# A butterfly with scaled sums on ScalarE, silu gates behind the transform, and a reordered output phase in an FNet and Hyena encoder layer

## The chip, the cores and the metric

One core of a Trainium2 chip runs the whole layer in one launch. The metric is the time of one execution in device microseconds. Five engines have queues of their own, each worked through in order: PE (TensorE, matmuls), DVE (VectorE), ACT (ScalarE), POOL (GpSimd) and SP, which here only issues DMAs. An instruction that waits holds back everything behind it in its own queue.

## The reference, cut to what matters

Two sequences of 1024 rows and 1024 channels pass through the same layer:

```
p = rmsnorm(x) @ w_in                     # split into fv, fg, hv (3 parts), hg, mg
y_f = (fft2(fv).real * silu(fg)) @ w_fourier_out
v, x1, x2 = short_conv(hv)                # width 3 along the sequence
z = v
for n, gate in enumerate((x1, x2)):
    z = gate * (irfft(rfft(z, 2L) * kf[:, n])[:L] + hyena_d[n] * z)
y_h = (z * silu(hg)) @ w_hyena_out
g_f, g_h = split(sigmoid(mg + b_merge))
out = x + rmsnorm((g_f * y_f + g_h * y_h) @ w_out)
```

`kf` is the spectrum of a filter that a small network makes from positions. All of it is fp32.

## The kernel before, in words

PE multiplies fp32 as a high and a low part. `split` (line 168) makes them: ACT casts the high part (line 171, "CAST" in the profile; the names end in h: wh, yh, bh), then DVE or POOL subtracts the low part (line 181; wl, yl, bl). `mm3` then needs three matmuls per product. So each operand passes through two engines before PE may use it.

The phases follow one another, the first index b being the sequence. (1) The Fourier branch, to 225 us. (2) 16 filter steps, to about 650 us; each makes one block of filter taps and transforms it. (3) `branches` (line 905): 32 convolution steps, 16 of b=0 to about 1110 us and 16 of b=1 to about 1700 us. Step i runs `conv_front` for i+1 (the transform's input), `gates` for i+1 (the multiplier `x` of the step, line 923), and then `conv_back` for i: matmuls into `pX`, DVE's products `t` and `y`, the split of `y` into `yh` and `yl`, and matmuls into `pT` that use these. (4) `phase_gates`, to about 1940 us: what is left of the gate projections, as block products with seven multiplications in place of eight ("jobs"). (5) `phase_out` (line 1095): for four units (b, half) the projections by w_fourier_out (`pyf`, operand `sf`) and w_hyena_out (`pyh`, operand `sh`), eight blocks `dt` each; each block loads two weight tiles `wr` by DMAs that POOL issues (line 1123), which `split` turns into `wh`, `wl`; then a sigmoid gate `g` is read back from DRAM by a DMA of SP (line 1151) and put through ACT (line 1153). (6) `last_rows` (line 1245), from 2302 us: eight jobs that multiply by w_out, again with seven multiplications, `po`, and write the rows.

`butterfly` (line 546) is called 48 times in the phases 2 and 3, once for each step. It takes the eight blocks of 128 columns of a transform's input (`xp`, and `xm` for the part that is subtracted: another tile in the 16 filter steps, `bs2` holding its sums; the same tile `xt` in the 32 convolution steps) and makes four groups b0 to b3 of four blocks. b1 and b3 are e ± C8·d and similar, eight `scalar_tensor_tensor` of 128 columns (line 177), each with the constant C8 inside. Groups 1 to 3 are split for the matmuls into `pX`.

In `gates`, the second convolution (n=1) of sequence 0 also multiplies `x` by silu of a gate. The gate lies in DRAM for the channels below NH; one half at a time, SP loads it into a tile "gt" of three buffers (line 935), ACT puts it through silu in place (line 937), and POOL multiplies. The silu is held behind `self.turned`, a mark of the filter phase.

What sets the order: a scheduler rearranges the program's instructions before they are fixed in each queue; `tc.issue_after(ins)` keeps an instruction behind a given one on its own engine, and costs no wait by itself. Tiles of one tag share their buffers, so that a new tile waits until the old one is used up. Two of these sharings matter: in `phase_gates`, `kept` (line 1052) puts copies of products in the tag "w" of two buffers, in which `phase_out` puts its first `wr`; the last copy is used up by the last `gt`.

`phase_out` prepares `last_rows` by the way: `beside` (line 1162) loads a block of w_out, splits it and its sums (`blocks`, line 1185), a quarter of the blocks at a time; in the last unit `sum4` (line 1208) loads the tiles T4 (`t4l`) from DRAM and splits them. In `last_rows`, `prepare` (line 1254) loads `mraw` by DMA and splits it for the next job; `kept` copies products out of PSUM (line 1286, `m` and `u`).

Of the kernel before, what the change touches and what calls it, by code (L numbers as in the profile page):

```python
# [161 lines left out]
class K:  # L162
# [5 lines left out]
    def split(self, h, l, src, eng="pool", heng="act"):  # L168
        nc = self.nc
        if heng == "act":  # L170
            self.rounded = nc.scalar.copy(h, src)  # L171
        else:
            nc.vector.tensor_copy(h, src)
        self.sub(eng, l, src, h)
# [4 lines left out]
    def tt(self, eng, out, a, b, op):  # L179
        e = self.nc.gpsimd if eng == "pool" else self.nc.vector  # L180
        e.tensor_tensor(out, a, b, op=op)  # L181
# [4 lines left out]
    def sub(self, eng, out, a, b):  # L186
        self.tt(eng, out, a, b, SUB)
# [359 lines left out]
    def butterfly(self, ws, xp, xm):  # L547
# [7 lines left out]
        b0, b2, b1, b3 = t("b0"), t("b2"), t("b1"), t("b3")  # L555
        out = {0: b0}

        def split(g, b):
# [3 lines left out]
            out[g] = (h, l)  # L562
        self.add("dve", s, xp[:, :, 0:2], xp[:, :, 2:4])
        self.add("dve", b0[:, 0::2], s[:, :, 0], s[:, :, 1])
        self.sub("dve", b0[:, 1::2], s[:, :, 0], s[:, :, 1])
        self.sub("dve", b2[:, 0:2], xp[:, 0, 0:2], xp[:, 0, 2:4])
        self.sub("dve", b2[:, 2], xp[:, 1, 3], xp[:, 1, 1])
        self.sub("dve", b2[:, 3], xp[:, 1, 0], xp[:, 1, 2])
        split(2, b2)
        if xm is xp:  # L570
            de, do, sgn = b2[:, 1], b2[:, 2], -1.0
            se, so = s[:, 0, 1], s[:, 1, 1]
        else:
# [333 lines left out]
    def branches(self, nb, nct, ws):  # L907
# [11 lines left out]
        Z, X = {}, {}  # L919
# [6 lines left out]
        def gates(i):  # L926
            b, n, c = steps[i]
            x = self.conv(2 + n, c, ws, f"x{n + 1}", b)
            if n and b == 0:
                early = c < NH  # L930
                ps = None if early else self.inproj(4, c)
                for q in range(2):
                    sg = self.wp.tile([P, 512], F32, tag="gt", name="sg", bufs=3)
                    if early:
                        nc.sync.dma_start(sg, self.d_g[0][4][c][:, 512 * q:512 * q + 512])
                    with tc.issue_after(self.turned.ins):
                        nc.scalar.activation(sg, sg if early else ps[:, 512 * q:512 * q + 512], AF.Silu)
                    self.mul("pool", x[:, 512 * q:512 * q + 512], x[:, 512 * q:512 * q + 512], sg)
            X[i] = x
        B = front(0)  # L940
        gates(0)
        for i, (b, n, c) in enumerate(steps):
# [6 lines left out]
            y = self.conv_back(n, c, B, ws)  # L949
            B = nxt  # L950
# [31 lines left out]
    def phase_gates(self):  # L982
# [6 lines left out]
        with ExitStack() as es:  # L989
# [62 lines left out]
            def kept(p, own=False):  # L1052
                t = gw.tile([P, 512], F32, tag="u", name="u", bufs=1) if own else wp.tile([P, 512], F32, tag="w", name="m", bufs=2)
# [12 lines left out]
            for i, (sec, c) in enumerate(jobs):  # L1066
# [6 lines left out]
                v = kept(pa)  # L1073
# [17 lines left out]
    def phase_out(self):  # L1091
# [6 lines left out]
        with ExitStack() as es:  # L1098
# [17 lines left out]
            def weight(w, dt, q):  # L1116
# [10 lines left out]
                self.weighed = self.rounded  # L1127
# [34 lines left out]
            def beside(i, dt):  # L1162

                with tc.issue_after(self.fetched.ins), tc.issue_after(self.opened.ins):
                    if i in (1, 2):
# [3 lines left out]
                        elif part == 3:  # L1169
                            blocks(k, self.raw)  # L1170
# [15 lines left out]
            def blocks(k, r):  # L1186
# [6 lines left out]
                self.sums(s, r)  # L1193
# [245 lines left out]
```

## Time and profile before

| | us |
|---|---|
| three runs, median | 2466.59 |
| lowest to highest | 2461.57 to 2469.35 |
| the profiled execution, its own time | 2470.75 |
| its span in the profile | 2469.0 |

The profiled execution lies 4.16 us above the median; 1.75 us of its time lie around the span. In the profile a row of a view gives an engine, a line of the kernel, the operation, out<-in by the names above and the shape. Where an engine stood idle before a row, brackets give the idle time and what ended it.

### The profile page before, as it was taken

The page shows a single profiled execution, that of the slowest core. Times are in us where ns is not written, and L with a number is a line of the kernel's source. Part 1 is how long each engine was busy: PE and PEld are TensorE (multiplying, and loading weights), DVE is VectorE, ACT ScalarE, POOL GpSimd, SP SyncE. Part 2 cuts the span into 40 slices and gives each one's busy share as a digit, 9 for nine tenths or more (in the row PEclk, how much of TensorE's full clock was granted, in tenths as well). Part 3 has the DMA queues.
Part 4 walks back from the last instruction along what each step waited for, and adds up shares of the span by engine and source line. Part 5 has one row for each costly group of instructions (what it writes and reads, how often), then busy time and mean ns, then how long its engine had stood idle before and what let it go on. Part 6 is the DMA issues. An engine that isn't in the chain of part 4 may idle for free.

```text
span 2469.0 us, 36969 instructions
## 1 busy us (share of the span) xinstructions
PE 2407.5 (98%) x13196; PEld 2086.9 (85%) x13196; DVE 1912.8 (77%) x3597; ACT 1064.4 (43%) x1919; POOL 499.0 (20%) x516
## 2 busy tenths in 40 slices
PE   6999999999999999999999999999999999999998
PEld 6988888888788888888888888888788788787786
DVE  7687898998649999899889999866556455665677
ACT  5546576766433333333222222323444344444343
POOL 1331213221342443331000000112100111112121
PEclk9999999999999999999999999999999999999999
DMA  7535655555555455545443443435444567775443
GB/s 274 183 122 205 217 182 166 169 180 168 171 174 179 159 176 163 172 149 203 137 134 131 143 142 131 133 128 176 161 162 158 193 218 255 237 268 194 156 160 128
DMA packets 225153, 429.37 MB, mean 174 GB/s; under 512 B 23542, under 2 KB 87255, under 8 KB 224456
## 3 DMA queue, kind: packets, MB, share of 16 engines
q1 hardware_dynamic: 198444, 333.34, 40.7%
q0 software_dynamic: 26336, 93.65, 10.7%
q8 instruction: 104, 1.70, 0.3%
q14 instruction: 81, 0.66, 0.1%
q10 hardware_dynamic: 188, 0.02, 0.0%
HBM read 290.60 MB, written 136.31 MB: 173 GB/s over the span
## 4 chain that ended last, share of the span: by engine, by line
PE 44%; DMA 4%; issue 4%; DVE 1%; POOL 1%; ACT 1%; SPq 0%; DVEq 0%; POOLq 0%; ACTq 0%
PE pin L194 17%; PE pg L194 8%; PE po L194 6%; PE pT L194 4%; PE pyf L194 4%; PE pX L194 4%; PE pyh L194 1%; DMA wr<-in_w_ho 1%; DMA wr<-in_w_fo 1%; POOL wr L1123 1%; PE tph L791 1%; DMA mraw<-d_m 1%; DMA d_m<-yf 1%; DMA t4l<-d_t 0%; DMA d_g<-gt 0%
## 5 line engine op out<-in xcount | busy, mean ns | idle before, releaser
L194 PE MATMUL pin<-xh,wl 128*128 128x512 f32 x1472 | 578.7, 393 | 3.3 <-POOL wl L181 3.3
L194 PE MATMUL pin<-xh,wh 128*128 128x512 f32 x1472 | 578.9, 393 | 1.1 <-DMA wh<-d_w 1.1
L194 PE MATMUL pin<-xl,wh 128*128 128x512 f32 x1472 | 577.5, 393 | 0.6 <-DVE xl L181 0.6
L181 POOL TENSOR_TENSOR wl<-wr,wh 128x512 fp32r<-128x512 f32 x136 | 246.2, 1811 | 1142.8 <-ACT wh L171 739.2
L194 PEld LDWEIGHTS pin<-xh,wl 128*128 128x128 f32 x1472 | 277.8, 189 | 54.9 <-POOL wl L181 4.1
L194 PEld LDWEIGHTS pin<-xl,wh 128*128 128x128 f32 x1472 | 277.7, 189 | 51.8 <-DVE xl L181 1.0
L194 PEld LDWEIGHTS pin<-xh,wh 128*128 128x128 f32 x1472 | 278.0, 189 | 51.3 <-DMA wh<-d_w 1.7
L171 ACT CAST wh<-wr 128x512 fp32r<-128x512 f32 x264 | 162.9, 620 | 326.1 <-PE pin L194 109.4
L194 PE MATMUL pT<-cinv,yh 128*128 128x256 f32 x1024 | 192.4, 283 | 4.4 <-ACT yh L171 4.4
L194 PEld LDWEIGHTS pT<-cinv,yh 128*128 128x128 f32 x1024 | 165.0, 191 | 13.9 <-ACT yh L171 4.9
L171 ACT CAST yh<-y 128x512 fp32r<-128x512 f32 x128 | 79.5, 621 | 202.5 <-DVE y L181 148.0
L181 DVE TENSOR_TENSOR t<-pX,k 128x1024 f32<-128x1024 f32 x128 | 155.5, 1215 | 14.2 <-PE pX L194 13.6
L194 PE MATMUL pyf<-sf,wh 128*128 128x512 f32 x512 | 159.1, 393 | 2.0 <-ACT wh L171 2.0
L194 PE MATMUL pX<-bh,cfwd 128*128 128x256 f32 x768 | 159.7, 286 | 0.0
L194 PE MATMUL pyh<-sh,wh 128*128 128x512 f32 x512 | 158.0, 390 | 1.6 <-ACT wh L171 1.6
L171 ACT CAST bh<-b 128x512 fp32r<-128x512 f32 x144 | 88.9, 619 | 135.1 <-DVE b L181 79.5
L181 DVE TENSOR_TENSOR wl<-wr,wh 128x512 fp32r<-128x512 f32 x128 | 87.4, 686 | 76.7 <-ACT wh L171 76.7
L194 PE MATMUL pT<-cinv,yl 128*128 128x256 f32 x512 | 145.3, 284 | 0.5 <-DVE yl L181 0.5
L194 PEld LDWEIGHTS pX<-bh,cfwd 128*128 128x128 f32 x768 | 125.8, 191 | 3.3
L194 PEld LDWEIGHTS pyf<-sf,wh 128*128 128x128 f32 x512 | 96.7, 189 | 22.8 <-ACT wh L171 2.8
L181 DVE TENSOR_TENSOR bl<-b,bh 128x512 fp32r<-128x512 f32 x144 | 102.6, 721 | 16.6 <-ACT bh L171 16.3
L194 PEld LDWEIGHTS pyh<-sh,wh 128*128 128x128 f32 x512 | 96.0, 188 | 22.2 <-ACT wh L171 2.5
(347 smaller groups left out, 5255.6 us busy)
## 6 DMA issues: line engine op xcount, KB each, us to landing
k<-d_k SPq DMA_DIRECT2D x128, 512.0 KB, 3.9
wr<-in_w_in SPq DMA_DIRECT2D x136, 256.0 KB, 3.1
d_g<-gt SPq DMA_DIRECT2D x124, 256.0 KB, 2.7
d_k<-kt SPq DMA_DIRECT2D x128, 128.0 KB, 2.2
d_k<-kt SPq DMA_DIRECT2D x64, 256.0 KB, 2.5
wr<-in_w_fo POOLq DMA_DIRECT2D x64, 256.0 KB, 3.3
g<-d_g SPq DMA_DIRECT2D x64, 256.0 KB, 3.7
wr<-in_w_ho POOLq DMA_DIRECT2D x64, 256.0 KB, 3.3
```

Source lines behind the costliest of these rows:

```text
L171: self.rounded = nc.scalar.copy(h, src)
L181: e.tensor_tensor(out, a, b, op=op)
L194: return self.nc.tensor.matmul(out, lhsT, rhs, start=start, stop=stop, skip_group_check=shared)
L791: nc.tensor.transpose(tp[:, q * P:(q + 1) * P], eo[:, e, q], self.ident)
L1123: nc.gpsimd.dma_start(r, a[w][dt][:, 512 * q:512 * q + 512])
```

## The change

**Butterfly.** Group b2 is made first. ACT then multiplies by ±C8 in place, in three instructions (of 256, 128 and 128 columns): the differences and the sums. b1 and b3 become one tile `b13` of eight blocks (b0 and b2 another, `b02`; the same memory), and DVE makes each pair of blocks by one `tensor_tensor` of 256 columns: four in place of eight.

**Silu gates.** SP's loads of both halves are issued first. For gates that lie in DRAM, silu and POOL's multiplication move into a new function `close(i + 1)`, called behind `conv_back(i)`; the silu is held behind that step's last cast on ACT.

**phase_gates.** The last job's product `v` is copied to a tile "f" in place of "w".

**phase_out and last_rows.** `beside` is held behind `weighed2` too, the last subtraction of a weight's `wl` on DVE. The sums of w_out's blocks have a part of their own, two `dt` later than the blocks. `sum4` only loads; T4's splits move into the first job of `last_rows`, behind a copy. `prepare` of the next job is held behind the copy `u`.

```diff
-        def t(name):
-            return ws.tile([P, 4, P], F32, tag="b", name=name, bufs=4)
+        b02, b13 = [ws.tile([P, 8, P], F32, tag="b", name=n, bufs=2) for n in ("b02", "b13")]
+        b0, b2, b1, b3 = b02[:, 0:4], b02[:, 4:8], b13[:, 0:4], b13[:, 4:8]
...
+        if xm is xp:
+            d, z = b2[:, 1:3], s
+            dn, dp = (0, 7), (3, 4)
+        else:
+            z = ws.tile([P, 2, 2, P], F32, tag="y", name="bs2", bufs=1)
+            self.add("dve", z[:, :, 1], xm[:, :, 1], xm[:, :, 3])
+            self.sub("dve", z[:, :, 0], xm[:, :, 1], xm[:, :, 3])
+            d = z[:, :, 0]
+            dn, dp = (0, 3), (4, 7)
+        nc.scalar.mul(z[:, :, 0], d, C8)
+        nc.scalar.mul(z[:, 0, 1], z[:, 0, 1], C8)
+        nc.scalar.mul(z[:, 1, 1], z[:, 1, 1], -C8)
         split(2, b2)
...
-        self.stt("dve", b1[:, 0], de, C8, e0)
-        self.stt("dve", b1[:, 3], do, C8 * sgn, o0)
-        self.stt("dve", b1[:, 1], se, C8, e2)
-        self.stt("dve", b1[:, 2], so, -C8, o2, MUL, SUB)
+        self.add("dve", at(*dn), xm[:, :, 0], z[:, :, 0])
+        self.add("dve", at(1, 6), z[:, :, 1], xm[:, :, 2])
+        self.sub("dve", at(*dp), xm[:, ::o, 0], z[:, ::o, 0])
+        self.sub("dve", at(2, 5), z[:, ::-1, 1], xm[:, ::-1, 2])
         split(1, b1)
-        self.stt("dve", b3[:, 0], de, -C8, e0)
-        self.stt("dve", b3[:, 3], do, -C8 * sgn, o0)
-        self.stt("dve", b3[:, 1], se, C8, e2, MUL, SUB)
-        self.stt("dve", b3[:, 2], so, -C8, o2)
...
+        def close(i):
+            if i in G:
+                sg, early = G.pop(i)
+                for q in range(2):
+                    s = slice(512 * q, 512 * q + 512)
+                    if early:
+                        with tc.issue_after(self.rounded.ins):
+                            nc.scalar.activation(sg[q], sg[q], AF.Silu)
+                    self.mul("pool", X[i][:, s], X[i][:, s], sg[q])
...
             y = self.conv_back(n, c, B, ws)
+            close(i + 1)
...
-                v = kept(pa)
+                v = kept(pa, last=i + 1 == len(jobs))
...
-                self.weighed = self.rounded
+                self.weighed, self.weighed2 = self.rounded, self.left
...
-                with tc.issue_after(self.fetched.ins), tc.issue_after(self.opened.ins):
+                with tc.issue_after(self.fetched.ins), tc.issue_after(self.opened.ins), tc.issue_after(self.weighed2.ins):
...
                         elif part == 3:
-                            blocks(k, self.raw)
+                            self.sum = blocks(k, self.raw)
+                        elif part == 5:
+                            sums(k, self.sum)
...
-                r = l.bitcast(F32)
-                nc.sync.dma_start(r, self.d_t[1][:, k])
-                self.split(h, l, r, "dve", "act")
+                nc.sync.dma_start(l.bitcast(F32), self.d_t[1][:, k])
...
             w = kept(pa, True)
+            fetched = self.copied
...
             if i + 1 < len(jobs):
-                A = prepare(i + 1)
+                with tc.issue_after(fetched.ins):
+                    A = prepare(i + 1)
                 pa, pb, m1 = first(A)
+            if i == 0:
+                with tc.issue_after(kept_v.ins):
+                    for h, l in T4:
+                        self.split(h, l, l.bitcast(F32), "dve", "act")
```

The scheduler also redraws the order around these edits. Three places show it. The first is ACT's queue in a step of `branches` of sequence 0, around a gate's silu (`sg`), `bh` being the cast of a butterfly's group and `yh` the cast that `pT` needs. Before:

```order
L171 CAST bh_11109<-b2_11100 128x512
L937 ACTIVATE sg_12103<-sg_12103 128x512
L171 CAST yh_11286<-y_11284 128x512
L171 CAST bh_11117<-b1_11101 128x512
L171 CAST wh_11788<-wr_11790 128x512
L758 ACTIVATE v_11704<-pin_11639,wsh_69 128x1024
L171 CAST yh_11324<-y_11322 128x512
```

And the same step with the change (its `bs` rows are the three new multiplications):

```order
L579 ACTIVATE bs_11295<-b02_11296 128x2x128
L580 ACTIVATE bs_11295<-bs_11295 128x128
L581 ACTIVATE bs_11295<-bs_11295 128x128
L171 CAST yh_11522<-y_11520 128x512
L951 ACTIVATE sg_11392<-sg_11392 128x512
L951 ACTIVATE sg_11393<-sg_11393 128x512
L839 COPY T1s_11501<-pT_11488 128x512
L171 CAST bh_11315<-b13_11297 128x512
L171 CAST bh_11319<-b13_11297 128x512
```

A silu that stood between two `yh` of a step stands behind its last `yh`, and both halves stand together.

The second place is ACT at the passage from `phase_gates` to `phase_out`: `wh` are the casts of the weight tiles, `g` the sigmoid gates. PE uses the tiles in the order of their numbers, before 20648, 20666, 20692, 20710, 20738, 20756 and with the change 20504, 20522, 20548, 20566, 20594, 20612; the third of each row is cast far ahead of this place. Before:

```order
L1054 COPY m_20553<-pg_20453 128x512
L171 CAST wh_20648<-wr_20646 128x512
L171 CAST wh_20756<-wr_20754 128x512
L171 CAST sh1_20728<-sh1_20728 128x512
L171 CAST wh_20666<-wr_20664 128x512
L171 CAST wh_20710<-wr_20708 128x512
L171 CAST sh0_20682<-sh0_20682 128x512
L1153 ACT_TABLE_LOAD
L1153 ACTIVATE g_20685<-g_20685,bm_70 128x512
L1153 ACTIVATE g_20731<-g_20731,bm_70 128x512
L171 CAST wh_20738<-wr_20736 128x512
L1153 ACTIVATE g_20777<-g_20777,bm_70 128x512
```

With the change (the first two weight casts, 20504 and 20522, stand ahead of this piece, among the casts of the last job):

```order
L1071 COPY v_20409<-pg_20309 128x512
L171 CAST wh_20566<-wr_20564 128x512
L171 CAST sh0_20538<-sh0_20538 128x512
L171 CAST wh_20594<-wr_20592 128x512
L1170 ACT_TABLE_LOAD
L1170 ACTIVATE g_20541<-g_20541,bm_70 128x512
L1170 ACTIVATE g_20587<-g_20587,bm_70 128x512
L171 CAST wh_20612<-wr_20610 128x512
L171 CAST sh1_20584<-sh1_20584 128x512
```

The fifth weight tile stood behind two gates and now stands ahead of them; the sixth, which stood second, is now behind them.

The third place is DVE's queue around the butterfly of the step shown first. Before, from its sums `bs` to the first rows of b1:

```order
L181 TENSOR_TENSOR bs_11098<-xt_11085 128x512
L181 TENSOR_TENSOR yl_11248<-y_11245,yh_11247 128x512
L177 SCALAR_TENSOR_TENSOR x2_11469<-pin_11404,wsh_69,x2_11469 128x1023
L177 SCALAR_TENSOR_TENSOR x1_10568<-yc_11009,invn_71,x1_10568 128x1024
L181 TENSOR_TENSOR b0_11099<-bs_11098 128x2x128 x2
L181 TENSOR_TENSOR b2_11100<-xt_11085 128x256
L181 TENSOR_TENSOR b2_11100<-xt_11085 128x128 x2
L177 SCALAR_TENSOR_TENSOR b1_11101<-bs_11098,xt_11085 128x128 x2
```

With the change:

```order
L181 TENSOR_TENSOR bs_11295<-xt_11282 128x512
L181 TENSOR_TENSOR yl_11485<-y_11482,yh_11484 128x512
L181 TENSOR_TENSOR U_11462<-T0s_11424,pT_11449 128x512
L177 SCALAR_TENSOR_TENSOR x2_10768<-yc_11274,invn_71,x2_10768 128x1024
L181 TENSOR_TENSOR b02_11296<-bs_11295 128x2x128 x2
L181 TENSOR_TENSOR y_11520<-t_11518 128x512
L181 TENSOR_TENSOR T0s_11424<-T0s_11424,pT_11449 128x512
L177 SCALAR_TENSOR_TENSOR x1_11736<-pin_11671,wsh_69,x1_11736 128x1023
L181 TENSOR_TENSOR b13_11297<-xt_11282,bs_11295 128x2x128
L181 TENSOR_TENSOR b13_11297<-xt_11282,bs_11295 128x256
L181 TENSOR_TENSOR b13_11297<-bs_11295,xt_11282 128x2x128 x2
```

Between the sums' last use on DVE (`b02<-bs`) and the first `b13`, three rows of other work now stand, while ACT's three multiplications run.

More of the change, by code (lines that the diff above doesn't have):

```diff
@@ L180, in tt @@
         e = self.nc.gpsimd if eng == "pool" else self.nc.vector
-        e.tensor_tensor(out, a, b, op=op)
+        return e.tensor_tensor(out, a, b, op=op)
     def add(self, eng, out, a, b):
@@ L186, in sub @@
     def sub(self, eng, out, a, b):
-        self.tt(eng, out, a, b, SUB)
+        return self.tt(eng, out, a, b, SUB)
     def mul(self, eng, out, a, b):
@@ L562, in split @@
             out[g] = (h, l)
+        self.sub("dve", b2[:, 0:2], xp[:, 0, 0:2], xp[:, 0, 2:4])
+        self.sub("dve", b2[:, 2], xp[:, 1, 3], xp[:, 1, 1])
+        self.sub("dve", b2[:, 3], xp[:, 1, 0], xp[:, 1, 2])
         self.add("dve", s, xp[:, :, 0:2], xp[:, :, 2:4])
@@ L931, in gates @@
                 ps = None if early else self.inproj(4, c)
+                sg = [self.wp.tile([P, 512], F32, tag="gt", name="sg", bufs=3) for q in range(2)]
                 for q in range(2):
-                    sg = self.wp.tile([P, 512], F32, tag="gt", name="sg", bufs=3)
+                    s = slice(512 * q, 512 * q + 512)
                     if early:
[L935 to L938, printed above, removed]
+                        nc.sync.dma_start(sg[q], self.d_g[0][4][c][:, s])
+                    else:
+                        nc.scalar.activation(sg[q], ps[:, s], AF.Silu)
+                G[i] = sg, early
             X[i] = x
+        def close(i):
+            if i in G:
+                sg, early = G.pop(i)
+                for q in range(2):
+                    s = slice(512 * q, 512 * q + 512)
+                    if early:
+                        with tc.issue_after(self.rounded.ins):
+                            nc.scalar.activation(sg[q], sg[q], AF.Silu)
+                    self.mul("pool", X[i][:, s], X[i][:, s], sg[q])
         B = front(0)
@@ L1050, in out, with kept @@
                 nc.sync.dma_start(self.d_g[b][sec][c][:, s], t)
-            def kept(p, own=False):
-                t = gw.tile([P, 512], F32, tag="u", name="u", bufs=1) if own else wp.tile([P, 512], F32, tag="w", name="m", bufs=2)
+            def kept(p, own=False, last=False):
+                if own or last:
+                    t = gw.tile([P, 512], F32, tag="u" if own else "f", name="u" if own else "v", bufs=1 if own else 3)
+                else:
+                    t = wp.tile([P, 512], F32, tag="w", name="m", bufs=2)
                 copied = nc.scalar.copy(t, p)
@@ L1193, in blocks, with sums @@
                 self.sums(s, r)
+                return s
+            def sums(k, s):
                 h, l = [bl.tile([P, 2, 512], F32R, tag=f"{t}{k}", name=f"{t}{k}", bufs=1) for t in ("th", "tl")]
@@ L1285, in kept @@
             t = wp.tile([P, 512], F32, tag="gt" if own else "w", name="u" if own else "m", bufs=3 if own else 2)
-            nc.scalar.copy(t, p)
+            self.copied = nc.scalar.copy(t, p)
             return t
```

23 lines of the change are left out of this document (6 added, 17 removed).

## The prediction

> **What bounds the kernel now.** I read the page first (busy time of each engine), then the windows by phase (window, us, busy time and count of PE, PEld, DVE, ACT and POOL, then PE's granted clock, DMA share, GB/s).
>
> ```profile
> PE 2407.5 (98%) x13196; PEld 2086.9 (85%) x13196; DVE 1912.8 (77%) x3597; ACT 1064.4 (43%) x1919; POOL 499.0 (20%) x516
> ...
> 0.00:225.00 225.00, 193.08 (x1485) 182.91 (x1486) 168.82 (x417) 123.01 (x247) 58.47 (x83) 0.98 0.58 200
> 600.00:700.00 100.00, 96.32 (x485) 81.29 (x484) 53.01 (x129) 46.35 (x90) 33.73 (x23) 0.98 0.55 181
> 700.00:1100.00 400.00, 395.55 (x2335) 350.09 (x2334) 365.11 (x600) 137.28 (x218) 145.78 (x141) 0.99 0.50 164
> 1100.00:1200.00 100.00, 98.44 (x580) 86.67 (x579) 97.26 (x160) 35.99 (x54) 13.96 (x12) 1.00 0.51 179
> 1940.00:2000.00 60.00, 57.95 (x245) 46.56 (x244) 26.87 (x42) 24.95 (x41) 11.26 (x21) 0.97 0.63 225
> 2000.00:2240.00 240.00, 237.59 (x1043) 195.08 (x1042) 148.03 (x225) 114.69 (x191) 46.68 (x87) 1.00 0.72 244
> 2240.00:2325.00 85.00, 81.21 (x346) 65.46 (x345) 47.04 (x71) 32.83 (x57) 14.54 (x26) 0.98 0.55 177
> 2325.00:2459.00 134.00, 133.99 (x592) 110.63 (x590) 102.09 (x211) 55.12 (x114) 27.60 (x24) 1.00 0.44 146
> ```
>
> PE sets the time: it is busy for 98%, and the change takes no matmul away. So time is won only where PE stands still, or runs at a lower clock behind a stall. About half of its idle time, 225 − 193 = 32 us, lies before 225 us, where nothing changes. Behind that, PE idles in a handful of places: 4.45 us in 700 to 1100, 2.05 in 1940 to 2000, 2.41 in 2000 to 2240, 3.79 in 2240 to 2325. DVE's 77% is the trap of this case: what the butterfly saves there is worth nothing unless PE waits for it.
>
> **The change part by part: silu gates (T1).** The only stall in 700 to 1100, in the timelines of PE, ACT and POOL:
>
> ```profile
> 989.97 0.79 PE L194 MATMUL pT<-cinv,yh 128*128 128x256 f32 x2 [4.45 <-ACT yh L171]
> 990.57 0.63 PE L194 MATMUL pin<-xh,wl 128*128 128x512 f32 x1
> ...
> 994.83 0.41 PE L194 MATMUL pin<-xh,wh 128*128 128x512 f32 x1
> ```
>
> ```profile
> 988.78 0.63 ACT L937 ACTIVATE sg<-sg 128x512 f32<-128x512 f32 x1 [7.13 <-DMA sg<-d_g]
> 989.32 0.60 ACT L171 CAST yh<-y 128x512 fp32r<-128x512 f32 x1
> ```
>
> ```profile
> 978.54 8.84 POOL L181 TENSOR_TENSOR x<-x,sg 128x512 f32<-128x512 f32 x2 [6.58 <-ACT wh L171]
> ```
>
> PE waited for `yh`, which stood on ACT behind a silu that waited 7.13 us for its gate's DMA; POOL held the gates' buffers for 8.84 us in two multiplications. Then ten matmuls from 990.57 to 994.83 took 0.426 us each; the usual distance is that of the window without idle time, 133.99 us / 592 = 0.227. So the place costs 4.45 + 10 × (0.426 − 0.227) = **6.5 us**. With the change the silu stands behind the step's last `yh`, and its load is issued a step earlier: behind it now wait `T1s` and two `bh`, which PE needs later. I credit all of it. If the load were as late again, this step has slack: a hold of 7.13 us cost PE 4.45, so a cast may be some 2.7 us late unnoticed.
>
> A rule of the Trainium skill bears on these ten matmuls ("TensorE: Matmul & The Clock Gate", Part 1): the array falls to half clock after an idle window of about 3.4 us, and cold starts at N=512 lie 426.7 ns apart. The trace agrees on the distance; on the threshold it does not, since T2 and T5 below restart slowly after 1.64 and 1.99 us. By the page only T1 would carry a restart, and the sum would be smaller by about 3.8 us; these rows speak against that.
>
> **Passage into phase_out (T2).**
>
> ```profile
> 1956.26 0.73 PE L194 MATMUL pyf<-sf,wh 128*128 128x512 f32 x2 [1.64 <-ACT wh L171]
> ...
> 1960.83 0.39 PE L194 MATMUL pyf<-sf,wl 128*128 128x512 f32 x1
> ```
>
> ```profile
> 1954.98 0.72 ACT L1153 ACTIVATE g<-g,bm 128x512 f32<-128x512 f32 x1 [2.88 <-DMA g<-d_g]
> 1955.61 0.60 ACT L171 CAST wh<-wr 128x512 fp32r<-128x512 f32 x1
> ```
>
> ```profile
> 1941.43 1.07 POOL L1123 DMA_DIRECT2D wr<-in_w_fo  x2 [9.74 <-DVE gt L181]
> ```
>
> The fifth weight tile's cast stood behind a gate that waited 2.88 us for its DMA; POOL's weight loads had waited 9.74 us for the buffer that `v` now leaves alone. Idle 1.64, then eleven matmuls in 4.57 us where 11 × 0.227 = 2.50 would do: **3.7 us**. With the change the loads start earlier, and this cast stands ahead of both gates. Late next is the sixth cast behind them; PE has 12 more matmuls, 2.7 us, before it, which covers the 1.64.
>
> **w_out's blocks (T3) and T4's tiles (T4).**
>
> ```profile
> 2098.47 1.05 ACT L171 CAST th<-osum 128x1024 fp32r<-128x1024 f32 x1
> 2099.42 1.14 ACT L171 CAST wh<-wr 128x512 fp32r<-128x512 f32 x2
> ...
> 2281.03 0.62 ACT L171 CAST t4h<-t4l 128x512 fp32r<-128x512 f32 x1 [5.52 <-DMA t4l<-d_t]
> 2281.55 0.61 ACT L171 CAST wh<-wr 128x512 fp32r<-128x512 f32 x1
> ```
>
> ```profile
> 2102.47 0.50 PE L194 MATMUL pyh<-sh,wl 128*128 128x512 f32 x1 [1.32 <-DVE wl L181]
> ...
> 2146.82 0.50 PE L194 MATMUL pyf<-sf,wl 128*128 128x512 f32 x1 [0.47 <-DVE wl L181]
> ...
> 2191.12 0.51 PE L194 MATMUL pyh<-sh,wl 128*128 128x512 f32 x1 [0.49 <-DVE wl L181]
> ...
> 2282.22 0.74 PE L194 MATMUL pyh<-sh,wh 128*128 128x512 f32 x2 [1.46 <-ACT wh L171]
> 2293.95 0.73 PE L194 MATMUL pyh<-sh,wh 128*128 128x512 f32 x2 [0.20 <-ACT wh L171]
> ```
>
> The block's 1024-column split stood ahead of a weight's in both queues; halved in two parts, and behind `weighed2`, it comes after. T3 is 1.32 + 0.47 + 0.49 = **2.3 us**. T4's cast waited 5.52 us ahead of a weight's cast; it leaves the phase: 1.46 + 0.20 = **1.7 us**. Its four casts now run in the first job of the last phase, 4 × 0.62 = 2.5 us of ACT, hidden there by an ACT that is busy 55 of 134 us.
>
> **last_rows (T5).**
>
> ```profile
> 2312.83 1.66 ACT L171 CAST wh<-mraw 128x512 fp32r<-128x512 f32 x3 [6.72 <-DMA mraw<-d_m]
> 2315.02 0.56 ACT L1286 COPY u<-po 128x512 f32<-128x512 f32 x1
> ```
>
> ```profile
> 2315.64 0.68 PE L194 MATMUL po<-t1h,mxh 128*128 128x512 f32 x1 [1.99 <-ACT u L1286]
> ...
> 2319.62 0.40 PE L194 MATMUL po<-t1l,mxh 128*128 128x512 f32 x1
> ```
>
> The copy `u` stood behind casts that waited 6.72 us for `mraw`; now they stand behind it. Idle 1.99, then ten matmuls in 3.98 us, not 2.27: **3.7 us**. Late next would be `wh` of job 1, which PE needs only behind this job's two remaining products; I charge nothing.
>
> **The butterfly.**
>
> ```profile
> L177 DVE SCALAR_TENSOR_TENSOR b<-bs,xt 128x128 f32<-128x128 f32 x128 | 34.2, 287 | 0.0
> L177 DVE SCALAR_TENSOR_TENSOR b<-b,xt 128x128 f32<-128x128 f32 x128 | 32.3, 291 | 1.2 <-PE pX L194 1.2
> ...
> L181 DVE TENSOR_TENSOR b<-bs 128x256 f32<-128x256 f32 x96 | 36.0, 413 | 0.1
> ...
> L686 ACT ACTIVATE kt<-kt 128x256 f32<-128x256 f32 x48 | 19.8, 413 | 18.0 <-DVE kt L177 17.2 <-ACT kt L686 0.6
> L700 ACT ACTIVATE kt<-kt 128x128 f32<-128x128 f32 x16 | 4.9, 305 | 2.9 <-DVE kt L177 2.9
> ```
>
> In a convolution step eight instructions took (34.2 + 32.3) / 32 = 2.08 us of DVE; four of 256 columns, at 36.0 / 96 each, take 1.50: 0.6 us saved, 32 × 0.6 = 19 us of DVE. ACT gets 0.413 + 2 × 0.305 = 1.0 us a step, 49 us in 48 steps. Neither is on PE's path: a `yh` behind the three comes 1.0 us later, within the 2.7 us of slack above. I credit and charge nothing for it.
>
> The order that the scheduler redraws in the filters and convolutions has no row. Its ends: a loss like T1's, 6.5 us, and as a gain the stall at 654 us and the idle time of 1100 to 1200:
>
> ```profile
> 653.99 0.79 PE L194 MATMUL pin<-xh,wl 128*128 128x512 f32 x1 [2.44 <-POOL wl L181]
> ...
> 646.21 8.96 POOL L181 TENSOR_TENSOR wl<-wr,wh 128x512 fp32r<-128x512 f32 x2 [5.42 <-ACT wh L171]
> ```
>
> that is 2.44 + 1.56 = 4.0 us. I charge 2, nearer to the loss: dozens of places can go wrong and two can mend. On the POOL row the Trainium skill says ("SBUF — State Buffer", Terms, shared port pair) that VectorE and GpSimd take turns at one port pair, a whole instruction each; the 8.96 us for two rows fit that. By it the new two-input additions lock POOL out as the old ones did, the 2.44 us cannot go, and the end of the gain would be 1.56 us, not 4.0.
>
> **Sum.** 6.5 + 3.7 + 2.3 + 1.7 + 3.7 = 17.9, less 2: 16 us. On the profiled execution, 2470.75 − 16 = 2454.75 (its span, 2469.0, and 1.75 around it). That execution stands 4.16 above the median of the three runs, so beside the median the forecast is **2450.6 us**.
>
> **Rivals.** *A: a stall comes back.* The redrawn order puts some cast that PE needs behind a waiting DMA elsewhere; one of T1's size gives 2457, two 2463.6. For it: 48 ACT trios are new in queues where one wait cost 6.5. Against: without T1 PE idles only 1.56 us in 700 to 1200, so the steps have slack. *B: the data are late anyway.* The gate at 1954.98 and `mraw` at 2312.83 landed late; if the earlier place of the casts only shows the next late operand, T2 and T5 stay: 2450.6 + 7.4 = 2458, with one A 2464.5. For it: the waits were long, 2.88 and 6.72 us. Against: PE's stalls were shorter than these. *C: slower.* In a step of sequence 0 DVE makes the sums, waits for ACT's three multiplications, and only then goes on; all its other work stands behind. DVE is idle there for (400 − 365.11) / 16 = 2.2 us a step and saves 0.6, so up to 2.8 us of wait a step is free. From then each microsecond costs 16: at 4.3 us the whole change is 8 us slower than before, at 5 us 16 × 2.2 − 16 = +19, 2486. For it: ACT was once held for 7.13. Against: three rows of other DVE work, 0.7 + 0.7 + 1.3 us by their kinds, stand in the gap, and ACT's trio takes 1.0. *D: it doesn't do what it says*: the same loads are late at other places, and all comes out as before, 2466.6.
>
> **How the numbers follow.** About 0.3%, 7.4 us, is what a measurement of this kernel can tell from no change. Forecast 0.58; A with one stall 0.12, with two 0.05; B 0.08, with A 0.02; C 0.07; D 0.08. Faster, below 2459.2: 0.58 + 0.12 + 0.08 = 0.78, a little off for sizes: 0.77. Slower 0.07, same 0.16. The range leaves out C and D and some 0.05 below: upwards to two stalls or B with A, 2464; downwards the forecast without the 2, and with the 4.0 gained, 2444.6, and 4 for the scatter of the median (2461.57 to 2469.35): 2440.
>
> **What would show it.** PE's idle time: none above 1 us at the gates of 700 to 1100, at the first weights of phase_out, behind w_out's blocks, at T4's loads and before the first `t1h`; window 700 to 1100 with PE near 400. ACT's rows of 579 to 581 near 0.4 and 0.3 us; DVE's `b13` without idle time before it above 1 us. Wrong would be: DVE idle before `b13` of over 2.8 us a step (C), a new PE stall released by `yh` or `bh` (A), `u` or the weights' casts with the old stalls (B).

## The result, and the profile after

The changed kernel takes 2444.94 us (median of six runs, 2443.13 to 2449.26) against 2467.52 us before, the two timed together: a ratio of 0.9912, 95% interval 0.9898 to 0.9927, so 22.6 us or 0.9% faster. The forecast was 2450.6 us, 16 us faster, with a range of 2440 to 2464. The direction, the range and most of the places held. Two terms did not: one gave nothing, and one that was charged with 2 us brought a gain.

The page's line of busy time and the windows by phase, of the kernel after:

```profile
PE 2396.1 (98%) x13196; PEld 2082.3 (85%) x13196; DVE 1893.8 (77%) x3405; ACT 1096.8 (45%) x2063; POOL 485.9 (20%) x516
...
600.00:700.00 100.00, 100.00 (x524) 86.05 (x524) 64.08 (x143) 55.25 (x111) 27.45 (x25) 1.00 0.60 199
700.00:1100.00 400.00, 400.00 (x2394) 355.74 (x2392) 372.04 (x570) 151.11 (x269) 146.71 (x145) 1.00 0.51 168
1100.00:1200.00 100.00, 97.56 (x561) 84.92 (x560) 92.27 (x142) 36.25 (x59) 7.32 (x4) 1.00 0.49 169
1940.00:2000.00 60.00, 60.00 (x267) 49.69 (x266) 31.38 (x49) 28.69 (x47) 11.79 (x23) 1.00 0.65 215
2000.00:2240.00 240.00, 237.80 (x1043) 194.96 (x1042) 145.85 (x223) 115.00 (x191) 46.58 (x87) 1.00 0.72 241
2240.00:2325.00 85.00, 85.00 (x376) 70.38 (x375) 54.21 (x89) 33.65 (x60) 17.15 (x25) 1.00 0.57 182
```

PE now fills the windows 700 to 1100, 1940 to 2000 and 2240 to 2325 wholly, as foretold, and its clock is 1.00 in each. It also fills 600 to 700, whose stall the forecast left standing. In 2000 to 2240 it idles 2.20 us, as good as the 2.41 before, and in 1100 to 1200 it idles 2.44, more than the 1.56 before.

Idle time leaves out the slow restart behind a stall. So for the comparison I add up PE's **lost time**: for each matmul the distance to the next start, less the usual distance for that kind of matmul in the same trace, summed over a window. All kernels of this study, by that sum (us; phases shift by up to some 30 us between kernels; the stalls at POOL's `wl` between 1710 and 1755 us so fall on either side of 1725, and the two columns around it are to be read together):

```
kernel       0-225 225-600 600-700 700-1100 1100-1725 1725-1900 1900-2000 2000-2240 2240-2325 | median, ratio to before
before        39.3   1.3     6.3     9.0       4.8       2.0       4.7       3.6       6.8
changed       41.0   1.5     0.1     1.4       6.7       1.1       0.3       3.6      -0.1   | 2444.94, 0.9912
bf_only       39.5   1.5     0.1     9.8       6.1       1.2       3.0       3.3       4.0   | 2461.25, 0.9975
silu_only     38.2   1.4     6.0     2.0       7.5       1.9       3.3       3.2       7.2   | 2464.05, 0.9983
late_only     37.6   1.4     4.3     9.5       4.3       3.0       1.2       3.3      -0.1   | 2457.63, 0.9955
old_bf        38.2   1.3     4.4     2.0       7.6       2.2       0.2       2.8      -0.1   | 2451.72, 0.9937
bf_cut        37.5   3.6     0.2     7.8       4.5       5.6       0.3       3.5      -0.1   | 2456.09, 0.9946
dve_scale     37.7   0.9     0.2     4.8       4.6      -0.2       0.6       4.8      -0.1   | 2447.19, 0.9908
b2_first      38.4   2.6     0.5     3.8       4.9       1.7       2.6       6.7       7.1   | 2457.57, 0.9957
old_b2first   38.2   2.5     0.5     1.4       4.2       1.6       0.2       2.7      -0.1   | 2445.37, 0.9911
no_t3         38.6   1.5     0.1     1.5       5.8       1.5      -0.1       5.4      -0.1   | 2447.53, 0.9912
wl_dve        38.1   1.2     0.3     1.8       3.6      -0.3       3.0       4.6       5.1   | 2453.44, 0.9945
prefetch      38.4   1.5     0.1     1.5       5.6       1.1       0.3      -0.4      -0.1   | 2441.84, 0.9892
plain_dve     39.2   1.5     0.1     1.4       3.1      -0.3       0.7      -0.4      -0.1   | 2437.99, 0.9883
```

From before to after the whole program's lost time falls from 77.7 to 55.3 us: 22.4, beside 21.9 between the two spans and 22.6 between the medians. The first window, in which nothing changes, differs by up to 4 us between profiles, and that is the grain of such sums; the profiled executions of before, of the changed kernel and of b2_first also lie some 4 us above their kernels' medians, that of wl_dve 2.6 below.

The butterfly's rows after, in the groups by form (busy us, mean ns, idle time before):

```profile
L181 DVE TENSOR_TENSOR b<-bs,xt 128x256 f32<-128x256 f32 x64 | 28.7, 485 | 0.0
L181 DVE TENSOR_TENSOR b<-xt,bs 128x256 f32<-128x256 f32 x64 | 25.1, 429 | 0.0
...
L580 ACT ACTIVATE bs<-bs 128x128 f32<-128x128 f32 x48 | 14.5, 301 | 1.1 <-DVE bs L181 1.1
L581 ACT ACTIVATE bs<-bs 128x128 f32<-128x128 f32 x48 | 14.3, 298 | 0.0
L579 ACT ACTIVATE bs<-b 128x256 f32<-128x256 f32 x32 | 13.2, 414 | 24.1 <-DVE b L181 24.0
```

ACT's three take 0.41 + 0.30 + 0.30 = 1.0 us a step, as worked out. DVE's four take (28.7 + 25.1) / 32 = 1.68 us a step, not 1.50: 0.4 us saved, not 0.6. DVE never waited ahead of them (0.0), so rival C did not come about.

### The profile page after: what moved, and what is told of

The parts are those of the page before. It is cut to its first block, busy times and chain, and to the rows that moved or that the text cites. A ratio compares the mean times of both kernels' runs of the same rounds, so it can differ in the third digit from the quotient of the medians.

```text
span 2447.1 us, 36853 instructions
## 1 busy us (share of the span) xinstructions
PE 2396.1 (98%) x13196; PEld 2082.3 (85%) x13196; DVE 1893.8 (77%) x3405; ACT 1096.8 (45%) x2063; POOL 485.9 (20%) x516
## 4 chain that ended last, share of the span: by engine, by line
PE 88%; DMA 5%; issue 3%; DVE 2%; ACT 1%; POOL 1%; SPq 0%; DVEq 0%; POOLq 0%; ACTq 0%
PE pin L194 41%; PE pT L194 7%; PE pg L194 7%; PE pX L194 7%; PE po L194 6%; PE pyh L194 5%; PE pyf L194 5%; PE pXf L194 3%; PE pfv L194 2%; DMA wr<-in_w_fo 1%; PE pft L194 1%; PE tph L792 1%; DMA wr<-in_w_ho 1%; PE tpx L194 1%; DMA wfv<-in_w_fv 1%
## 5 line engine op out<-in xcount | busy, mean ns | idle before, releaser
L181 POOL TENSOR_TENSOR wl<-wr,wh 128x512 fp32r<-128x512 f32 x136 | 240.3, 1768 | 1144.0 <-ACT wh L171 1105.9
L194 PE MATMUL pX<-bl,cfwd 128*128 128x256 f32 x384 | 109.6, 285 | 0.0
```

The source lines that it names most:

```text
L181: return e.tensor_tensor(out, a, b, op=op)
L194: return self.nc.tensor.matmul(out, lhsT, rhs, start=start, stop=stop, skip_group_check=shared)
```

## The experiments

**The parts one by one.** Four kernels take the change apart. `bf_only` is the kernel before with the new `butterfly`; `silu_only` is it with the new `branches`; `late_only` is it with the edits behind 1700 us alone; `old_bf` is the changed kernel with the old `butterfly`:

```diff
# bf_only: kernel before
-    def butterfly(...)   # of before
+    def butterfly(...)   # of the change
# silu_only: kernel before
-    def branches(...)    # of before
+    def branches(...)    # of the change
# late_only: changed kernel, butterfly(...) and branches(...) of before
# old_bf: changed kernel, butterfly(...) of before
```

> The kernel before with the new butterfly alone. Theory 1 (the butterfly takes away the stall at the end of the filter phase, 6.2 us of PE's lost time in 600 to 700 us, and nothing else): 6 us faster, about 2461, PE at 100 of 100 us in that window; the silu stall near 985, the two at 1956, and those at 2282 and 2315 stay. Theory 2 (the butterfly is off PE's path, as the prediction had it, and the stall went by the order that the other edits drew): within 2 us of before, PE near 96 of 100 us in 600 to 700.

> The kernel before with the moved silu gates alone. Theory 1 (each stall belongs to its own edit): PE's stall near 985 goes, 4.45 of idle time and 2.0 to 2.5 of slow restart: 7 us faster, about 2460.5; 600 to 700 keeps its stall (PE 96 of 100 us). Theory 2 (the stall at 985 was an accident of the order and moves with any edit): a stall of some 4 us with a slow restart stands at another place of 700 to 1110 us, within 2 us of before.

> The kernel before with the edits behind 1700 us alone (the tile of the last product, the sums apart and behind wl, T4's splits moved, prepare behind the copy u). Theory 1: the stalls at 1956, 2282 and 2315 go, 4.2 + 3.0 + 3.9 us of lost time, and that of w_out's blocks only moves: 11 us faster, about 2456.5, and up to 1700 us the trace is that of before. Theory 2 (the gate's data and mraw would be late anyway, and came in time only because the whole program ahead ran otherwise): the stalls at 1956 and 2315 stay, 3 us faster.

> The changed kernel with the old butterfly put back. Theory 1 (the butterfly is worth the 6.2 us at the end of the filters): 6 us slower than the changed kernel, about 2451 (16 faster than before), PE near 96 of 100 us in 600 to 700. Theory 2 (the butterfly is worth nothing): 2445, as the changed kernel, PE near 100 of 100 us there.

Measured: bf_only 2461.25 us, ratio 0.9975 (0.9965 to 0.9986); silu_only 2464.05, 0.9983 (0.9971 to 0.9995); late_only 2457.63, 0.9955 (0.9940 to 0.9970); old_bf 2451.72, 0.9937 (0.9920 to 0.9955). The windows of bf_only, silu_only and late_only, in this order:

```profile
600.00:700.00 100.00, 100.00 (x524) 86.11 (x523) 63.28 (x144) 57.07 (x114) 26.66 (x25) 1.00 0.60 194
700.00:1100.00 400.00, 394.64 (x2336) 348.27 (x2335) 382.69 (x560) 145.49 (x259) 135.55 (x140) 1.00 0.52 164
```

```profile
600.00:700.00 100.00, 96.81 (x483) 81.67 (x482) 52.34 (x126) 43.75 (x85) 33.62 (x24) 0.98 0.56 181
700.00:1100.00 400.00, 400.00 (x2376) 354.92 (x2375) 376.10 (x610) 139.60 (x225) 158.49 (x144) 1.00 0.52 167
1100.00:1200.00 100.00, 96.23 (x564) 84.43 (x563) 97.26 (x161) 34.85 (x52) 8.69 (x7) 1.00 0.52 177
```

```profile
600.00:700.00 100.00, 96.66 (x492) 81.67 (x491) 51.55 (x124) 45.47 (x88) 34.56 (x24) 1.00 0.58 186
700.00:1100.00 400.00, 395.39 (x2332) 350.11 (x2331) 369.04 (x606) 136.98 (x219) 144.90 (x140) 0.99 0.51 164
```

Each stall goes with its own part. The filters' stall goes with the butterfly (100.00 against 96.8 and 96.7), the one at 985 with the silu gates, and those of 1900 to 2000 and of 2240 to 2325 with the late edits (lost time 11.5 before, 1.1 in late_only; the kernels that keep the late code of before lose 7.0 to 11.5 there). silu_only, late_only and old_bf have the filters in the order of before on every engine, and all three keep that stall: 2.17, 2.33 and 2.18 us idle, against 2.44. silu_only wins less than the 7 us expected, since a new stall begins near 1105 us (lost time 4.8 to 7.5 in 1100 to 1725): part of the gain is given back at the passage to sequence 1. The parts' gains by their ratios, 6.2 + 4.2 + 11.1 = 21.5 us, add up to the whole change's 22. So theory 1 holds for the parts' worth, with one exception within them: in bf_only the stall at 985 shrank to 1.2 us of lost time, and several small ones at late DVE rows stand for it, 9.8 us in 700 to 1100 as against 9.0 before. The prediction's "nothing" for the butterfly's part is wrong by some 6 us. What in the butterfly did it was open.

**What of the butterfly freed the filters.** Two kernels part its two effects. `bf_cut` cuts the four paired additions into eight of 128 columns; `dve_scale` makes the scaled sums on DVE:

```diff
# bf_cut: changed kernel; so for each of the four
-        self.add("dve", at(*dn), xm[:, :, 0], z[:, :, 0])
+        for e in range(2):
+            self.add("dve", at(*dn)[:, e], xm[:, :, 0][:, e], z[:, :, 0][:, e])
# dve_scale: changed kernel; so for each of the three
-        nc.scalar.mul(z[:, :, 0], d, C8)
+        nc.vector.tensor_scalar(z[:, :, 0], d, C8, None, op0=MUL)
```

> The changed kernel, its four additions of 256 columns cut into eight of 128: ACT's round trip stays, DVE's saving is gone. Theory S (what ends the stall at the end of the filters is the gap that ACT's round trip leaves in DVE's row of SBUF-only work, into which rows with a PSUM operand come, and there POOL gets its turn): the stall stays away, PE at 100 of 100 us in 600 to 700, within 3 us of the changed kernel, 2443 to 2448. Theory D (it is DVE's saved time): the 6 us come back, about 2451, PE near 96 of 100 us.

> The changed kernel with the three scalings on DVE: no round trip through ACT, and DVE about as long in a butterfly as before. Theory S: DVE's SBUF-only rows of a filter step stand in one piece again, POOL's wl is held for over 5 us, and the stall at the end of the filters is back, 4 to 6 us slower than the changed kernel, 2449 to 2451. Theory D: the same here, since no time is saved; the two part on the other kernel. If PE stays at 100 of 100 us in 600 to 700, both fall, and the place was freed by the redrawn order alone.

Measured: bf_cut 2456.09 us, ratio 0.9946 (0.9930 to 0.9963); dve_scale 2447.19, 0.9908 (0.9872 to 0.9943). The stall at the end of the filters stays away in both (lost time 0.2). bf_cut has the round trip and no saving, dve_scale has neither, and both are free of it: theories S and D fall together. dve_scale is as fast as the changed kernel, with nothing for ACT to do. bf_cut is slower for other reasons: it loses 7.8 us in 700 to 1100, mostly to `t` and `yl` rows of DVE that come late, and 5.8 at POOL's two `wl` near 1727 and 1735 us, against 3.0 at those of the changed kernel. That is the price of one draw of the order, one arrangement that the scheduler came to; whether the eight rows or the draw bring it, this run can't tell.

What was left was the order alone. `b2_first` is the kernel before with three subtractions written ahead of three additions and subtractions of the sums, and the same work on every engine. `old_b2first` is the changed kernel with that old butterfly:

```diff
# b2_first: kernel before; old_b2first: changed kernel with the butterfly of before
+        self.sub("dve", b2[:, 0:2], xp[:, 0, 0:2], xp[:, 0, 2:4])
+        self.sub("dve", b2[:, 2], xp[:, 1, 3], xp[:, 1, 1])
+        self.sub("dve", b2[:, 3], xp[:, 1, 0], xp[:, 1, 2])
         self.add("dve", s, xp[:, :, 0:2], xp[:, :, 2:4])
...
-        self.sub("dve", b2[:, 0:2], xp[:, 0, 0:2], xp[:, 0, 2:4])
-        self.sub("dve", b2[:, 2], xp[:, 1, 3], xp[:, 1, 1])
-        self.sub("dve", b2[:, 3], xp[:, 1, 0], xp[:, 1, 2])
```

> The kernel before, its butterfly making b2 ahead of the sums and nothing else changed: the same instructions on the same engines, in an order that the scheduler draws anew from the first filter step on. Theory R (the stall at the end of the filters is an accident of the order, freed by any new draw that lets POOL's wl fall elsewhere against DVE's SBUF-only run): PE at 100 of 100 us in 600 to 700, 3 to 6 us faster than before if nothing is lost elsewhere. Theory B (it needs the new butterfly's instructions): the stall stays, PE at 95 to 97 of 100 us, within 2 us of before.

> The changed kernel with the butterfly of before (eight rows of 128 columns on DVE, nothing on ACT), only its b2 made ahead of the sums. Theory R (the order alone freed the place; the scaled sums on ACT and the paired additions are worth nothing): within 2 us of the changed kernel, 2443 to 2447, PE at 100 of 100 us in 600 to 700, and 5 to 8 us faster than the changed kernel with the butterfly put back unaltered (2451.7). Theory B (the new butterfly's work itself counts, DVE being busy for 372 of 400 us in the convolutions of sequence 0): 4 to 8 us slower than the changed kernel, 2449 to 2453, PE losing time in 700 to 1100 to late rows of DVE.

Measured: b2_first 2457.57 us, ratio 0.9957 (0.9943 to 0.9972): ten us for moving three lines. old_b2first 2445.37, 0.9911 (0.9897 to 0.9924), the changed kernel's time to the half microsecond. The windows of b2_first, then of old_b2first:

```profile
600.00:700.00 100.00, 99.95 (x523) 85.60 (x522) 68.65 (x163) 55.43 (x107) 32.02 (x24) 1.00 0.60 197
700.00:1100.00 400.00, 398.35 (x2376) 353.48 (x2375) 380.64 (x622) 140.46 (x225) 159.58 (x144) 1.00 0.51 166
```

```profile
600.00:700.00 100.00, 99.95 (x524) 85.61 (x523) 67.53 (x163) 53.54 (x104) 31.93 (x24) 1.00 0.60 197
700.00:1100.00 400.00, 400.00 (x2393) 355.53 (x2392) 381.39 (x624) 142.56 (x229) 161.99 (x145) 1.00 0.52 168
```

Theory R holds: the filters' stall was an accident of the order. But the four new orders of the filters that lack it (those of bf_only, bf_cut, dve_scale and b2_first) all make b2 first, so whether any new order would do, or this move alone, stays open. With the old silu code b2_first also loses the stall at 985 (1.65 us idle in 700 to 1100, not 4.45), so that one hung on the order too: the moved silu removes it, but another draw does as well. The scaled sums on ACT and the paired additions are worth nothing that stands out of the differences between orders: without them, in a good order, the kernel takes 2445.37 against 2444.94.

**What the accident was.** DVE's rows before, at the stall (from the timeline; start, us, count at the row's end), while POOL's row of 8.96 us at 646.21, shown in the prediction, ran:

```profile
646.02 0.68 DVE L181 TENSOR_TENSOR xp<-fO 128x512 f32<-128x512 f32 x1
...
649.91 1.70 DVE L177 SCALAR_TENSOR_TENSOR b<-bs,xm 128x128 f32<-128x128 f32 x8
651.53 1.28 DVE L181 TENSOR_TENSOR bl<-b,bh 128x512 fp32r<-128x512 f32 x2
```

And POOL and DVE after, at the answering place:

```profile
651.82 1.68 POOL L181 TENSOR_TENSOR wl<-wr,wh 128x512 fp32r<-128x512 f32 x1 [7.50 <-ACT wh L171]
...
651.92 0.42 DVE L181 TENSOR_TENSOR b<-xp 128x256 f32<-128x256 f32 x1
652.26 1.00 DVE L177 SCALAR_TENSOR_TENSOR kt<-pXf,th,ktmp 128x256 f32<-128x256 f32 x3
```

Before, DVE ran from 646.0 to 652.8 without a gap, and all its rows have both inputs in SBUF. POOL's first subtraction, begun at 646.21, was done at 653.9, 1.1 us behind that run, and PE waited. After, rows that read a product out of PSUM (`pXf`) stand in the run, and the same subtraction takes 1.68 us. The Trainium skill ("SBUF — State Buffer", SBUF: two separate sides) says that a VectorE instruction with two SBUF inputs and a GpSimd instruction that reads SBUF exclude each other for one whole instruction. The trace agrees on which rows shut POOL out. It differs on how long: POOL was kept out not for one row but for the whole run of them, 20 instructions back to back. The prediction wrote that by this rule the 2.44 us could not go. But the rule says what a collision costs; which rows collide, and whether PE needs the result then, is the order's doing. POOL is held for over 4 us four to seven times in the filters of each of these orders, and only in that of before does one such hold stop PE for over 1 us. In b2_first one of 5.33 us (the first of two instructions here) ends at 661.13, and PE, busy until then, takes the weight at 661.19:

```profile
655.80 7.02 POOL L181 TENSOR_TENSOR wl<-wr,wh 128x512 fp32r<-128x512 f32 x2 [7.52 <-ACT wh L171]
```

The stall at 985 began with the same collision. DVE's rows before, while POOL's two multiplications `x<-x,sg` of 978.54, shown in the prediction, ran, and SP's wait for them (us in total, times, longest, of the whole execution):

```profile
978.32 1.27 DVE L177 SCALAR_TENSOR_TENSOR x<-yc,invn,x 128x1024 f32<-128x1024 f32 x1
...
984.35 0.68 DVE L181 TENSOR_TENSOR bl<-b,bh 128x512 fp32r<-128x512 f32 x1
984.95 1.21 DVE L181 TENSOR_TENSOR t<-pX,k 128x1024 f32<-128x1024 f32 x1
...
SPq L935 <- POOL x L181: 30.6, 8, 12.2
```

Until 984.95 all these rows have both inputs in SBUF, and there is no gap. POOL's first multiplication took 7.62 us, to 986.16, the second 1.26. SP issued the next gate's load at 986.19, when the first had freed its buffer; the silu, `yh` and PE waited in turn. In bf_only and b2_first, which have the old silu code, the two take 1.29 and 1.74 us in this step, and the stall of 4.45 us is gone. So the moved silu takes `yh` out from behind a late gate, and another order takes away the lateness.

POOL holds DVE in the same way. The silu edit moves POOL's multiplication for every gate, also for those that don't lie in DRAM. In silu_only two of these (1099.87 to 1102.41) hold a DVE row of 512 columns for 3.15 us in place of 0.68, ahead of the new stall near 1105; in the changed kernel two (1131.57 to 1134.38) hold two DVE rows for 1.52 us each in place of 0.41, ahead of one at 1134.

A test of the collision itself puts the low parts of the gates' weights on DVE, in the kernel before:

```diff
-                self.split(*parts, r, "pool", "act")
+                self.split(*parts, r, "dve" if b is None else "pool", "act")
```

> The kernel before, with the low parts of the gates' weights (the POOL subtractions of the filter phase and of the plain gates) made by DVE. Theory L (POOL is shut out while DVE runs rows without a PSUM operand): a wl takes 0.7 us on DVE in place of 1.3 to 8 on POOL, the stall released by POOL's wl at 651 goes, PE's idle time in 600 to 700 falls from 3.7 to under 1.5 us. Rival (DVE, with 333 of 375 us busy in the filters, is too full): DVE's 0.7 us rows come late instead, PE waits for wl on DVE, and the time is that of before or above it, 2466 to 2475.

Measured: 2453.44 us, ratio 0.9945 (0.9928 to 0.9961). PE's lost time in 600 to 700 falls from 6.3 to 0.3; a DVE too full for it did not show. POOL makes no `wl` in the filters there. It fits theory L, but the order is redrawn here as well, and the stall at 985 goes too (1.8 in 700 to 1100), so this run alone does not separate the two.

**The term that gave nothing.** ACT's waits in 2000 to 2240 (us in total, times, longest), before and after:

```profile
ACT g L1153 <- DMA g<-d_g: 14.9, 7, 3.8
```

```profile
ACT g L1170 <- DMA g<-d_g: 36.1, 16, 5.8
```

And the place after where a block of w_out still stops PE:

```profile
2181.67 0.72 ACT L1170 ACTIVATE g<-g,bm 128x512 f32<-128x512 f32 x1 [3.95 <-DMA g<-d_g]
2182.30 1.04 ACT L171 CAST th<-osum 128x1024 fp32r<-128x1024 f32 x1
2183.24 1.14 ACT L171 CAST wh<-wr 128x512 fp32r<-128x512 f32 x2
...
2185.85 0.50 PE L194 MATMUL pyh<-sh,wl 128*128 128x512 f32 x1 [1.18 <-DVE wl L181]
```

ACT waits for a gate's DMA; behind it stand the sums' cast and then the weights'. The wait for the block was exchanged for one for the gate. Two kernels try this: `no_t3` undoes the two edits, `prefetch` loads each gate one `dt` ahead, which puts its DMA in front of the write `d_m` on SP, which waits for DVE:

```diff
# no_t3: changed kernel
-                with tc.issue_after(self.fetched.ins), tc.issue_after(self.opened.ins), tc.issue_after(self.weighed2.ins):
+                with tc.issue_after(self.fetched.ins), tc.issue_after(self.opened.ins):
...
-                            self.sum = blocks(k, self.raw)
-                        elif part == 5:
-                            sums(k, self.sum)
+                            sums(k, blocks(k, self.raw))
# prefetch: changed kernel; the load of g leaves gated() for fetch()
+            def fetch(i, sec, dt):
+                if dt == 8:
+                    i, sec, dt = (i, 6, 0) if sec == 5 else (i + 1, 5, 0)
+                if i < len(units):
+                    b, half = units[i]
+                    GT[i, sec, dt] = wp.tile([P, 512], F32, tag="gt", name="g", bufs=3)
+                    self.fetched = nc.sync.dma_start(GT[i, sec, dt], self.d_g[b][sec][dt][:, 512 * half:512 * half + 512])
...
-                g = wp.tile([P, 512], F32, tag="gt", name="g", bufs=3)
-                self.fetched = nc.sync.dma_start(g, self.d_g[b][sec][dt][:, 512 * half:512 * half + 512])
+                g = GT.pop((i, sec, dt))
...
                     g = gated(i, dt, ps, 6, 8 + dt, None)
+                    fetch(i, 6, dt + 1)
```

> The changed kernel with w_out's blocks and their sums in one part again and without the wait behind wl (the term T3 of the prediction undone). Theory 1 (these edits won nothing, because gates that wait for their DMA now stand ahead of the weights' casts): within 1.5 us of the changed kernel, PE's lost time in 2000 to 2240 near 3.7 us as in the changed kernel. Theory 2 (they won the 2.3 us, and another edit brought new stalls): 2.3 us slower, 2447, lost time near 6.

> The changed kernel with each gate of phase_out loaded one dt ahead, before the write of d_m that SP waits for. Theory 1 (the late loads of the gates are what holds the weights' casts on ACT): ACT's wait for g's DMA in 2000 to 2240 falls from 36 us to under 10, PE's lost time there from 3.7 to under 1.5 us, 2 us faster than the changed kernel, about 2443. Theory 2 (the transfers themselves are late, the DMA engines being busy for 0.72): ACT's wait stays over 25 us and the time at 2445.

Measured: no_t3 2447.53 us, ratio 0.9912 (0.9883 to 0.9941); prefetch 2441.84, 0.9892 (0.9863 to 0.9921). The lost time of no_t3 in the window is 5.4, nearer to theory 2, of the changed kernel 3.6, of before 3.6. In this order the edits are worth 1.8 us, though ACT's wait for gates is 36.1 us with them and 20.5 without. By the runs' times this is not resolved, and the order moves the window as much: the other kernels without the edits lose 3.2 to 6.7 us there, those with them (prefetch and plain_dve aside) 2.7 to 4.8. Nor is prefetch told from the changed kernel by its time; but in its trace nothing is left:

```profile
2000.00:2240.00 240.00, 240.00 (x1060) 198.72 (x1060) 147.93 (x223) 116.84 (x192) 48.42 (x90) 1.00 0.73 246
...
ACT g L1178 <- DMA g<-d_g: 12.1, 14, 1.9
```

ACT's wait for gates is down to 12.1 us, longest 1.9 (expected were under 10), and PE fills the window. The DMA engines, at 0.73, are as busy as before, so it was the issue that came late, not the transfer.

**A faster version.** The changed kernel still stands at 1712 and 1730 us for POOL's `wl`. Its POOL rows there, the first with two instructions, and a row of DVE at each:

```profile
1710.82 5.08 POOL L181 TENSOR_TENSOR wl<-wr,wh 128x512 fp32r<-128x512 f32 x2 [5.79 <-ACT wh L171]
1728.52 2.85 POOL L181 TENSOR_TENSOR wl<-wr,wh 128x512 fp32r<-128x512 f32 x1 [5.92 <-ACT wh L171]
...
1710.26 2.29 DVE L181 TENSOR_TENSOR tl<-xsum,th 128x2048 fp32r<-128x2048 f32 x1 [1.98 <-ACT th L171]
1727.96 2.29 DVE L181 TENSOR_TENSOR tl<-xsum,th 128x2048 fp32r<-128x2048 f32 x1 [1.98 <-ACT th L171]
```

`plain_dve` is prefetch with the low parts of these last gates' weights on DVE:

```diff
-                self.split(*parts, r, "pool", "act")
+                self.split(*parts, r, getattr(self, "wl_eng", "pool"), "act")
...
+            self.wl_eng = "dve"
             for sec, c in plain:
                 self.spill_gate(1, sec, c, ws)
```

> The kernel with the gates loaded ahead, and the low parts of the last plain gates' weights (from about 1690 us) made by DVE. Theory L: the two stalls released by POOL's wl near 1710 and 1728 us (1.04 + 1.03 us idle, and their slow restart) shrink, since a wl of 0.7 us stands right behind DVE's long subtraction and needs no turn: 0.5 to 2 us faster than with the gates ahead alone, 2440 to 2441.5. Rival: wl waits in DVE's queue behind the sums' rows, and the stalls stay or grow: 2442 to 2444.

Measured: 2437.99 us, ratio 0.9883 (0.9868 to 0.9899), so 1.17% faster than before and, by the two ratios, 0.29% or some 7 us faster than the changed kernel. Against prefetch alone the intervals overlap, and the gain is read from the traces. This is the cleaner test of the collision: up to about 1690 us the order is that of prefetch. `wl` takes 0.69 us on DVE:

```profile
1714.64 2.29 DVE L181 TENSOR_TENSOR tl<-xsum,th 128x2048 fp32r<-128x2048 f32 x1 [1.98 <-ACT th L171]
1716.85 0.68 DVE L181 TENSOR_TENSOR wl<-wr,wh 128x512 fp32r<-128x512 f32 x1
```

Lost time in 1100 to 1725 falls from 5.6 to 3.1 and in 1725 to 1900 from 1.1 to nothing, 3.9 us together, beside 3.85 between the medians; both of POOL's stalls are gone. They account for 2.7 us, somewhat more than expected. The other 1.2 lie at a weight's load near 1140 us, where both kernels have the same order, and are no gain of this edit.

## Why the prediction was right, and where it was not

- **What bounds the kernel**: right. All 22.4 us are lost time of PE; its matmuls are the same 13196.
- **T1, silu gates, 6.5 us**: right in size, 7.0 to 7.6 in 700 to 1100. That it belongs to the silu's place alone is not: b2_first has the old place and not the stall. The prediction saw POOL's 8.84 us and did not ask what held POOL.
- **T2, 3.7 us, and T4 with T5, 5.4 us**: right mechanism, each somewhat small: 4.4 and 6.9. These are prices of one order and one execution: with the late code of before, T2's window loses 2.6 to 4.7 us in the five traces and that of T4 and T5 4.0 to 7.2. `u` now runs ahead of the casts of `mraw`, in ACT's rows after, and the slow restart is gone with the stall:

```profile
2293.31 0.59 ACT L1306 COPY u<-po 128x512 f32<-128x512 f32 x1 [1.25 <-PE po L194]
2293.80 1.14 ACT L171 CAST wh<-mraw 128x512 fp32r<-128x512 f32 x2
```

- **T3, 2.3 us**: wrong: 0 between before and after, and the 1.8 by no_t3 is within what the order moves. The step that failed is "halved in two parts, and behind `weighed2`, it comes after": it did not ask what would stand ahead of the weights' casts then. It was the gate that waits for its DMA, which is rival B at a place where the prediction did not look for it.
- **The order redrawn, charged with 2 us**: wrong in sign. The filters' 6.2 us came for nothing, and 1100 to 1900 took 1.0 back: a gain of about 5. Set against the charge of 2 this is 7 us, about the forecast's shortfall; T3's miss and the small sizes of the other terms nearly cancel. The step that failed is the choice "nearer to the loss: dozens of places can go wrong and two can mend". A stall that hangs on one collision at one moment need not be met again in a new order: bf_only, bf_cut, dve_scale and b2_first, four draws of the filters' order, all lost it, though all four make b2 first.
- **The butterfly itself, nothing**: right, for a reason that had to be shown. Its part brought 5.5 us by bf_only, but old_b2first has the same time without its work.
- **Rivals**: B's data were not late (T2 and T5 went whole), C did not happen, D neither. A did not come as told: the new stalls, near 1105 us in silu_only and at 1134 in the changed kernel, stand behind DVE rows that POOL held, not behind a cast that waits for a DMA.

## What to carry to other kernels

Where a scheduler redraws the order, an edit's gain is not its own until the same order, or another without the edit, has been timed: here moving three lines gave 10 us, and the scaled sums on ACT gave none that could be measured. Look ahead of each wait that is taken away for the next one in the same queue, and ask when its DMA is issued, not only where its consumer stands. Small subtractions that PE waits for do not belong on GpSimd beside a VectorE that runs long rows out of SBUF.

## What the runs showed of the hardware that was not expected

- POOL's subtraction of 512 columns takes 1.3 us where DVE leaves it room, 2.85 us when it starts 0.56 us into a DVE row of 2.29 us, and 7.7 us when DVE runs 6.8 us of rows with both inputs in SBUF; DVE makes the same in 0.69. Two of POOL's multiplications held a DVE row of 0.68 us for 3.15.
- Whether PE restarts slowly does not follow from the idle time alone. It did after 1.64 us (before, T2: eleven matmuls in 4.57 us), and did not after 2.40 us (wl_dve, before `t1h`). At the end of the filters, in one and the same order, it did after 2.44 and 2.17 us (before, silu_only) and did not after 2.33 and 2.18 (late_only, old_bf). What decides it was not tried.
